# Rotary tables that carry the row factors, and values transposed by DMA in a one-layer convolution and retention kernel

## The chip, the cores and the metric

The kernel runs on one core of one Trainium2 chip. A core has five engines that each run their own instructions in order and wait for one another through semaphores: PE (matrix products, with its weight loads shown apart as PEld), DVE (vector operations), ACT (element-wise functions and copies), POOL (a second, slower vector engine) and SP, which here only issues transfers (DMAs). SBUF is the memory on the chip that all of them work in, PSUM the banks that PE writes. The metric is the device time of one execution in microseconds. Three runs of the kernel before took 887.11, 887.15 and 887.49 us; the median is 887.15.

## The reference

One layer of a hybrid mixer over 2064 rows (16 learned "meta" rows, then 2048 input rows) of 1024 features. Four heads of chunked retention and four groups of gated convolution share one input projection and one output projection.

```python
def mixer_layer(h, norm_g, w_in, conv_w, ret_norm_g, w_out, pos):
    hn = rms_norm(h, norm_g)
    proj = jnp.einsum('bld,de->ble', hn, w_in)
    cx, cb, cc, cg, q, k, v, rg = jnp.split(proj, N_PROJ, axis=-1)
    conv_out = short_conv_branch(cx, cb, cc, conv_w) * jax.nn.silu(cg)
    qf = rotary(q.reshape(shp), pos) * (RET_HEAD_DIM ** -0.5)
    kf = rotary(k.reshape(shp), pos)
    ret = head_group_norm(retention_chunkwise(qf, kf, vf), ret_norm_g)
    ret_out = ret * jax.nn.silu(rg)
    mixed = jnp.concatenate([conv_out, ret_out], axis=-1)
    return h + jnp.einsum('ble,ed->bld', mixed, w_out)
```

In retention, a chunk of 128 rows has `scores = (q k^T) * decay`, an inner part `scores v`, a cross part from a running state, and the state gets `k^T v` of the chunk. `head_group_norm` then takes away each row's mean and divides by its spread, with a small constant EPS under the root. A last RMS norm closes the layer. `rms_norm` divides a row by the root of its mean square: that factor, one number a row, is called the row factor below.

## The kernel before

**Rows and passes.** The 2048 rows are worked in two passes (`r` = 0, 1) of 1024 rows; a pass has two halves (`j` = 0, 1) of 512. Everything is kept with features in the 128 partitions and rows along the free axis. The row factor isn't applied to the input; it is put in later, where it is cheap.

**Products.** A "unit" is one head or one convolution group. Each unit has two "quads". A quad computes two feature tiles (128 features) for both halves. `quad` (lines 206 to 241) does it with seven products instead of eight, in Strassen's manner: sums of weights on one side, sums of inputs on the other, three banks. Each product is 12 matmuls, since each operand is split into a rounded part and a rest (`mh`/`ml` for the inputs, `wh`/`wl` for the weights). After products 0, 2 and 3 ACT copies a bank (`copy`, L222, tile `tc`); `take` then gets what belongs to tile `i` (0 or 1) and half `j`: for three of the four a bank and a copy that DVE adds, for the last, `take(1, 0, xb, None)`, a bank alone. Where the summed inputs aren't ready yet, `quad_plain` (L254) does eight plain products.

**Feeding PE.** SP loads four raw weight tiles (`ra`, eight buffers, L439), POOL makes the sums (`sa`, `ra`, L111 and L114), ACT casts each to `wh` (L102), DVE subtracts to get `wl` (L114). `wh` and `wl` have three buffers each, so the cast for a product can run once the product three before it has left PE.

**A head** (`head`, L596). The first quad gives keys and values: `take` (L603) writes `kv` tiles and turns the keys with `rotary` (L571), four DVE instructions that read the tables `rot_t`. The second quad gives queries, turned likewise, and gates (tile `qg`), which are multiplied by the row factor and put through Silu. Then, for each half: PE transposes the keys chunk by chunk (L654), ACT scales them to `kd` (L656), PE transposes the values (L659), ACT writes them back times the squared row factor (L663), PE makes the state updates (L669). After that scores (L682), the decay mask (L684), inner and cross parts (L692, L693) and the group norm follow. A normalised tile `y` is turned to the feature layout by `turn` (L714): ACT splits 32-bit words into two planes of 16 bits (L716), a transposing DMA moves the planes (L717, `across<-apart`), and later ACT joins them (`finish`, L722). `turn` and `finish` wait in two lists and are worked off by `catch_up` in the two quads of the next unit, each tied behind a bank copy.

**What sets the order.** The program is written unit by unit, and a list scheduler that simulates the engines orders the instructions of each engine ahead of time; `tc.issue_after(ins)` puts what is in its block behind `ins` on the same engine. The order on an engine is then fixed, and a late instruction holds up all that follow it there. The tiles `kv`, `qg`, `u`, `x`, `t` and others share 16 buffers (`gen`).

**Row factors.** `row_factors` (L347) sums squares on ACT; `spread_factors` (L326) makes the factor `rc` (POOL's power, L281), spreads it over the partitions with a diagonal and PE (`spread`, L284, tile `rot`, L295) into `rr` and, squared, `rr2`, and returns the square `rc2` by row and `ev`, the EPS term of the group norm. In the first pass this happens while plain products run, just ahead of the first head.

Of the kernel before, what the change touches and what calls it, by code (L numbers as in the profile page):

```python
# [15 lines left out]
P = 128  # L16
# [55 lines left out]
def hybrid_trunk(ctx: ExitStack, tc: tile.TileContext, t, out: bass.AP, chunk_decay):  # L72
# [132 lines left out]

    def quad(w, m, take):


        def product(i, bank, first):
            (wh, wl) = w[i]  # L210
            for kt in range(KH):
                ks = slice(kt * P, (kt + 1) * P)
                mh, ml = m[i][kt]
                for n, (a, b) in enumerate(((wl, mh), (wh, ml), (wh, mh))):
                    nc.tensor.matmul(  # L215
                        bank, a[:, ks], b, start=first and kt == 0 and n == 0, stop=kt == KH - 1 and n == 2,
                        skip_group_check=not first,
                    )

        def copy(bank):  # L220
            c = sb.tile([P, HB], F32, name="tc", tag="tc", bufs=COPIES)
            copied[0] = nc.scalar.copy(out=c, in_=bank)  # L222
            return c

        xb = ps_proj()
        product(0, xb, True)
        c = copy(xb)
        yb = ps_proj()
        product(1, yb, True)
        take(0, 0, yb, c)  # L230
        product(2, xb, False)
        u2 = copy(xb)
        zb = ps_proj()
        product(3, zb, True)
        c = copy(zb)
        product(4, xb, False)
        take(1, 1, xb, c)
        product(5, zb, False)
        take(0, 1, zb, u2)
        product(6, xb, False)  # L240
        take(1, 0, xb, None)
# [84 lines left out]
    def spread_factors(ss, rr, rr2):  # L326
# [3 lines left out]
        rc = small.tile([P, CH], F32, name="rc", tag="rc")  # L330
        v = rsqrt_mean(rc, ss[:, 0, :])
        spread(rc, P, rr, rr2)
        rc2 = small.tile([P, CH], F32, name="rc2", tag="rc2", bufs=2 * NR)
        nc.vector.tensor_tensor(out=rc2, in0=rc, in1=rc, op=ALU.mult)
# [3 lines left out]
            in0=eps_col.rearrange("p (h c) -> p h c", c=1).broadcast_to([P, NG, CH]),  # L338
            in1=v.rearrange("p (h c) -> p h c", h=1).broadcast_to([P, NG, CH]),
            op=ALU.mult,  # L340
        )
        return rc2, ev

# [239 lines left out]
    def planes(a):  # L583
        return a.bitcast(U16).rearrange("p (two n) -> p two n", two=2)

    waiting = [[], []]

# [8 lines left out]
    def head(h, r, m, rot_t, f, turning, blocks, ahead, first=(), between=()):  # L596


        between = iter(between)
        k, v = [None, None], [None, None]  # L600
        tables = [rot_t[:, :, j * HB : (j + 1) * HB] for j in range(2)]

        def take(i, j, pp, c):  # L603
            d = gen("kv")[:, :HB]
            if c is None:
                nc.scalar.copy(out=d, in_=pp)
            else:
                add(nc.vector, d, pp, c)
            if i == 0:
                rotary(d, tables[j])  # L610
                k[j] = d
            else:
                v[j] = d

        if len(first) > 0:
# [7 lines left out]
        def take(i, j, pp, c):  # L623
# [8 lines left out]
            else:  # L632
# [3 lines left out]
                nc.vector.tensor_tensor(out=d, in0=pp, in1=f[0][:, j * HB : (j + 1) * HB], op=ALU.mult)  # L636
                nc.scalar.activation(d, d, AF.Silu)
                sg[j] = d
# [3 lines left out]
        else:  # L642
            quad(stationary(load_raw(w_loads(2 * h + 1))), m, take)
            catch_up(1)
        next(between, lambda: None)()
        if blocks[1]:
# [4 lines left out]
        for j in range(2):  # L651
# [4 lines left out]
            nc.scalar.mul(kd, tp, kd_col[:, h : h + 1])  # L656
            tp = ps_misc()
            for c in range(CH):
                nc.tensor.transpose(tp[:, c * P : (c + 1) * P], v[j][:, c * P : (c + 1) * P], ident)  # L659
            vj = v[j]  # L660
            for c in range(CH):
                cs = slice(c * P, (c + 1) * P)
                nc.scalar.mul(vj[:, cs], tp[:, cs], f[2][j][0][:, c : c + 1])  # L663
            vt.append(vj)
# [13 lines left out]
        for j in range(2):  # L678
# [22 lines left out]
            rs = small.tile([P, CH, 1], F32, name="rs", tag="rs")  # L701
            ev = f[2][j][1]
            add(nc.vector, rs, mv[:, :, 1:2], ev[:, h, :].rearrange("p (c a) -> p c a", a=1))
# [9 lines left out]

            def turn(j=j, y=y, apart=turning[0][:, j * HB : (j + 1) * HB], across=turning[1][:, j * HB : (j + 1) * HB]):  # L714

                nc.scalar.copy(out=planes(apart), in_=halves(y))  # L716
                nc.sync.dma_start(  # L717
                    across.bitcast(U16).rearrange("p (c f) -> p c f", c=2 * CH), apart.bitcast(U16), transpose=True
                )

# [94 lines left out]
    for r in range(NR):  # L815
# [4 lines left out]
        def load_tables():  # L820
            nc.sync.dma_start(rot_t, t["rot"][:, :, p0 : p0 + BLK])

        if r == 0:
            w = [None] * 4
# [21 lines left out]
            for _ in row_factors(0, f):  # L846
                pass
            nc.sync.dma_start(causal, t["causal"])
            nc.sync.dma_start(conv_w, t["conv_w"])
# [9 lines left out]
        else:  # L859
            m, b = moving(load_x(r), gain_of)  # L860
            first = [plain_parts(w_loads(0))]
            load_tables()
            prepared(m, sums_x, (1, 3))
            between = (lambda: prepared(m, sums_x, (0, 2)),)
# [75 lines left out]
```

## Time and profile before

| | |
|---|---|
| median of three runs | 887.15 us |
| the profiled execution | 886.64 us |
| its span, first to last instruction | 884.9 us |
| DMA queue 1, share of 16 engines | 43.0% |
| mean granted PE clock | 0.999 |

In the rows that the prediction shows, a group is "line engine operation out<-in shapes xcount | busy us, mean ns of one | idle time just before them, and what ended it". A row of the timeline is "start, length, engine, line, operation, count, and in brackets the idle time before it". A row of the chain of waits is "start, length, what", and each piece is the work that the next piece had to wait for. PE's matmuls overlap in the pipeline: a matmul's own length is longer than the step from one to the next.

### The profile page before, as it was taken

The page shows a single profiled execution, that of the slowest core. Times are in us where ns is not written, and L with a number is a line of the kernel's source. Part 1 is how long each engine was busy: PE and PEld are TensorE (multiplying, and loading weights), DVE is VectorE, ACT ScalarE, POOL GpSimd, SP SyncE. Part 2 cuts the span into 40 slices and gives each one's busy share as a digit, 9 for nine tenths or more (in the row PEclk, how much of TensorE's full clock was granted, in tenths as well). Part 3 has the DMA queues.
Part 4 walks back from the last instruction along what each step waited for, and adds up shares of the span by engine and source line. Part 5 has one row for each costly group of instructions (what it writes and reads, how often), then busy time and mean ns, then how long its engine had stood idle before and what let it go on. Part 6 is the DMA issues. An engine that isn't in the chain of part 4 may idle for free.

```text
span 884.9 us, 12802 instructions
## 1 busy us (share of the span) xinstructions
PE 872.3 (99%) x4343; PEld 717.7 (81%) x4343; DVE 718.4 (81%) x1176; ACT 441.1 (50%) x848; POOL 400.4 (45%) x291
## 2 busy tenths in 40 slices
PE   8999999999999999999999999999999999999996
PEld 5778788878888878888888888888888887788885
DVE  6888888989877866999899999877768699767763
ACT  8664426354545463836352534444334475555553
POOL 0554232323235554452223333354546445887773
PEclk9999999999999999999999999999999999999999
DMA  9721216455334343834236363325222493545531
GB/s 338 234 65 50 73 49 180 142 152 170 90 101 145 107 144 95 288 113 135 58 85 215 88 223 96 119 71 155 60 72 60 145 366 108 175 159 175 171 129 74
DMA packets 93137, 121.12 MB, mean 137 GB/s; under 512 B 24528, under 2 KB 41232, under 8 KB 93072
## 3 DMA queue, kind: packets, MB, share of 16 engines
q1 hardware_dynamic: 93072, 120.31, 43.0%
q8 instruction: 34, 0.56, 0.3%
q14 instruction: 31, 0.25, 0.1%
HBM read 90.92 MB, written 25.17 MB: 131 GB/s over the span
## 4 chain that ended last, share of the span: by engine, by line
PE 56%; DVE 6%; DMA 2%; issue 2%; ACT 1%; POOL 1%; SPq 0%; POOLq 0%; DVEq 0%; ACTq 0%
PE pj L215 50%; DVE ml L114 2%; PE pj L265 2%; DVE wl L114 1%; PE ms L682 1%; PE ms L669 1%; DVE ml L106 1%; PE ms L693 1%; PE ms L692 1%; DMA t<-sums_w 1%; DMA n<-in_x 1%; POOL yo L111 0%; DMA yo<-in_x 0%; DMA ra<-in_w_in 0%; DVE pm L709 0%
## 5 line engine op out<-in xcount | busy, mean ns | idle before, releaser
L215 PE MATMUL pj<-mh,wl 128*128 128x512 f32 x1008 | 398.7, 396 | 1.9 <-ACT tc L222 1.0
L215 PE MATMUL pj<-ml,wh 128*128 128x512 f32 x1008 | 393.2, 390 | 0.0
L215 PE MATMUL pj<-mh,wh 128*128 128x512 f32 x1008 | 392.7, 390 | 0.0
L102 ACT CAST wh<-ra 128x512 fp32r<-128x512 f32 x216 | 133.7, 620 | 260.9 <-PE pj L215 201.3
L215 PEld LDWEIGHTS pj<-mh,wl 128*128 128x128 f32 x1008 | 189.3, 188 | 44.7 <-ACT tc L222 2.8
L114 DVE TENSOR_TENSOR wl<-ra,wh 128x512 fp32r<-128x512 f32 x216 | 193.4, 898 | 39.3 <-ACT wh L102 38.9
L215 PEld LDWEIGHTS pj<-mh,wh 128*128 128x128 f32 x1008 | 189.2, 188 | 39.8
L215 PEld LDWEIGHTS pj<-ml,wh 128*128 128x128 f32 x1008 | 189.4, 188 | 37.9 <-issue 0.5
L114 POOL TENSOR_TENSOR ra<-ra 128x512 f32<-128x512 f32 x72 | 113.1, 1571 | 93.9 <-PE ms L400 40.9
L111 POOL TENSOR_TENSOR sa<-ra 128x512 f32<-128x512 f32 x36 | 55.2, 1533 | 100.0 <-DVE wl L114 46.7
L114 POOL TENSOR_TENSOR ra<-sa,ra 128x512 f32<-128x512 f32 x36 | 52.5, 1459 | 92.5 <-DVE wl L114 78.2
L222 ACT COPY tc<-pj 128x512 f32<-128x512 f32 x108 | 62.8, 581 | 0.0
L265 PE MATMUL pj<-ml,mh 128*128 128x512 f32 x128 | 50.2, 392 | 0.1
L265 PE MATMUL pj<-mh,mh 128*128 128x512 f32 x128 | 49.9, 393 | 0.0
L265 PE MATMUL pj<-mh,ml 128*128 128x512 f32 x128 | 48.8, 398 | 0.5 <-DVE ml L114 0.4
L525 POOL TENSOR_TENSOR c<-c,rr 128x512 f32<-128x512 f32 x14 | 27.8, 1984 | 26.8 <-DVE c L525 18.0
L705 POOL TENSOR_TENSOR rp<-rs,neg_half 128x4 f32<-128x4 f32 x16 | 19.4, 1215 | 43.4 <-DVE rs L111 43.4
L756 DVE TENSOR_TENSOR yo<-pj,yo 128x512 f32<-128x512 f32 x32 | 21.9, 687 | 17.9 <-PE pj L215 8.0
L102 ACT CAST wh<-sa 128x512 fp32r<-128x512 f32 x36 | 22.4, 621 | 27.5 <-PE pj L215 27.4
L761 POOL TENSOR_TENSOR z<-yo,final_g 128x512 f32<-128x512 f32 x16 | 27.0, 1687 | 16.1 <-DVE yo L756 16.1
L525 POOL TENSOR_TENSOR c<-c,tc 128x512 f32<-128x512 f32 x14 | 25.5, 1823 | 17.8 <-ACT tc L552 17.8
L758 ACT ACTIVATE rot<-yo 128x512 f32<-128x512 f32 x32 | 20.2, 630 | 26.8 <-DVE yo L756 25.8
(137 smaller groups left out, 1166.0 us busy)
## 6 DMA issues: line engine op xcount, KB each, us to landing
ra<-in_w_in SPq DMA_DIRECT2D x128, 256.0 KB, 2.7
x<-in_xT SPq DMA_DIRECT2D x48, 256.0 KB, 4.8
w<-in_w_out SPq DMA_DIRECT2D x32, 256.0 KB, 4.7
ra<-mixed SPq DMA_DIRECT2D x32, 256.0 KB, 2.9
yo<-in_x SPq DMA_DIRECT2D x32, 256.0 KB, 4.6
ra<-in_x SPq DMA_DIRECT2D x16, 256.0 KB, 3.2
mixed<-c SPq DMA_DIRECT2D x16, 256.0 KB, 2.5
mixed<-qg SPq DMA_DIRECT2D x16, 256.0 KB, 2.4
```

What stands on the lines that cost most here:

```text
L102: nc.scalar.copy(out=hi, in_=src)
L106: nc.vector.scalar_tensor_tensor(out=lo, in0=src, scalar=scale, in1=hi.bitcast(F32), op0=ALU.mult, op1=ALU.subtract)
L111: eng.tensor_tensor(out=out, in0=a, in1=b, op=ALU.add)
L114: eng.tensor_tensor(out=out, in0=a, in1=b, op=ALU.subtract)
L215: nc.tensor.matmul(bank, a[:, ks], b, start=first and kt == 0 and n == 0, stop=kt == KH - 1 and n == 2, skip_group_check=not first,)
L222: copied[0] = nc.scalar.copy(out=c, in_=bank)
L265: nc.tensor.matmul(banks[i], a[:, ks], b, start=half + kt + n == 0, stop=half == 1 and kt == KH - 1 and n == 2,)
L525: eng.tensor_tensor(out=out, in0=a, in1=b, op=ALU.mult)
L705: nc.gpsimd.tensor_tensor(out=rp, in0=rs, in1=neg_half.rearrange("p (c a) -> p c a", a=1), op=ALU.pow)
L756: last[0] = nc.vector.tensor_tensor(out=y, in0=pp, in1=y, op=ALU.add)
L758: nc.scalar.activation(junk, y, AF.Square, accum_out=ss[:, i, j : j + 1])
L761: nc.gpsimd.tensor_tensor(out=ys[i][j], in0=y, in1=final_g[:, j * HB : (j + 1) * HB], op=ALU.mult)
```

## The change

Three things are done together.

1. `scale_tables` multiplies both rotary tables by the squared row factor `rr2`, in place, on POOL, once a pass and half. Keys and queries so carry the squared row factor from the rotary on. For the keys this stands in for the factor that the values had; for the queries it is one number a row, and the group norm takes it out again, with `ev` now made from `rc2`.
2. The values need no factor any more, and PE no longer transposes them. `part` splits a value tile into planes on ACT (tile `pl`), and a transposing DMA moves it (tile `tr`). The value tile of half 0 is split right from its bank, in `take`; that of half 1 is first added up by DVE and then split behind the second quad's first bank copy (`split_late`). `join` puts the planes together on ACT (tile `v`): half 0 behind the second quad's second copy, half 1 behind its last copy. At the second pass's first head, whose first quad is plain, both are split from their banks.
3. The gates' Silu moves from the second quad to `turn`, in the next unit.

```diff
-    def quad(w, m, take):
+    def quad(w, m, take, steps=()):
+        steps = iter(steps)
...
+        def step():
+            with tc.issue_after(copied[0].ins):
+                next(steps, lambda: None)()
+
         xb = ps_proj()
         product(0, xb, True)
         c = copy(xb)
+        step()
...
         product(2, xb, False)
         u2 = copy(xb)
+        step()
...
+    def cross(across, apart):
+        nc.sync.dma_start(
+            across.bitcast(U16).rearrange("p (c f) -> p c f", c=2 * CH), apart.bitcast(U16), transpose=True
+        )
+
+    def part(a):
+        apart, across = gen("pl")[:, :HB], gen("tr")[:, :HB]
+        nc.scalar.copy(out=planes(apart), in_=halves(a))
+        cross(across, apart)
+        return across
...
         def take(i, j, pp, c):
+            if i == 1 and c is None:
+                v[j] = part(pp)
+                return
...
-                nc.scalar.activation(d, d, AF.Silu)
...
-            quad(stationary(load_raw(w_loads(2 * h + 1))), m, take)
+            def split_late():
+                for j in late:
+                    v[j] = part(v[j])
+
+            def join(j):
+                a = gen("v")[:, :HB]
+                nc.scalar.copy(out=halves(a), in_=planes(v[j]))
+                v[j] = a
+
+            quad(stationary(load_raw(w_loads(2 * h + 1))), m, take, (split_late, lambda: join(0)))
             catch_up(1)
+            with tc.issue_after(copied[0].ins):
+                join(1)
...
-            tp = ps_misc()
-            for c in range(CH):
-                nc.tensor.transpose(tp[:, c * P : (c + 1) * P], v[j][:, c * P : (c + 1) * P], ident)
             vj = v[j]
-            for c in range(CH):
-                cs = slice(c * P, (c + 1) * P)
-                nc.scalar.mul(vj[:, cs], tp[:, cs], f[2][j][0][:, c : c + 1])
...
+                nc.scalar.activation(sg[j], sg[j], AF.Silu)
...
+        def scale_tables():
+            for j in range(2):
+                a = rot_t[:, :, j * HB : (j + 1) * HB]
+                b = f[1][:, j * HB : (j + 1) * HB].rearrange("p (a n) -> p a n", a=1)
+                nc.gpsimd.tensor_tensor(out=a, in0=a, in1=b.broadcast_to([P, 2, HB]), op=ALU.mult)
```

In the first pass `scale_tables()` stands behind `row_factors`, in the second behind `load_tables()`.

How the instructions move on an engine is shown at three places. On PE, after the second quad of the first pass's first head (`ms` is a PSUM bank, `ident` the identity of the transposes, `pj` a product's bank), before:

```order
L215 MATMUL pj<-mh_358,wh 128x512
L400 MATMUL ms<-ra,meta_s 16x128 x8
L654 MATMUL ms<-ident,kv 128x128 x4
L659 MATMUL ms<-ident,kv 128x128 x4
L215 MATMUL pj<-mh_115,wl 128x512
```

And now, where the keys' transposes are L688 and a product is L217:

```order
L217 MATMUL pj<-mh_358,wh 128x512
L408 MATMUL ms<-ra,meta_s 16x128 x8
L688 MATMUL ms<-ident,kv 128x128 x4
L217 MATMUL pj<-mh_115,wl 128x512
L217 MATMUL pj<-ml_116,wh 128x512
```

The four value transposes between the keys' and the next product are gone; the same holds at all 16 such places.

On POOL, ahead of the first pass's first head (`rc` is the power of the second half's row factors, `u` and `carry` belong to the convolution, `sa` and `ra` are the weight sums of the head's first quad), before:

```order
L111 TENSOR_TENSOR sa<-ra 128x512
L281 TENSOR_TENSOR rc<-rs_v,neg_half 128x4
L454 COPY u<-u 128x2
L453 COPY u<-carry_78 128x2
L114 TENSOR_TENSOR ra<-ra 128x512
L456 COPY carry_78<-u 128x2
L114 TENSOR_TENSOR ra<-sa,ra 128x512
```

And now:

```order
L111 TENSOR_TENSOR sa<-ra 128x512
L289 TENSOR_TENSOR rc<-rs_v,neg_half 128x4
L855 TENSOR_TENSOR rot_t<-rot_t,rr_363 128x2x512
L462 COPY u<-u 128x2
L461 COPY u<-carry_78 128x2
L114 TENSOR_TENSOR ra<-ra 128x512
L855 TENSOR_TENSOR rot_t<-rot_t,rr_363 128x2x512
L464 COPY carry_78<-u 128x2
L114 TENSOR_TENSOR ra<-sa,ra 128x512
```

The two table multiplies stand ahead of the weight sum `ra<-sa,ra`.

On SP, at the second pass's first head (`mixed` is a store of the unit before, `t` are summed inputs for products 3 and 4 of the head's second quad, counted from 0), before:

```order
L447 DMA mixed_89<-c 128x4x128
L447 DMA mixed_88<-c 128x4x128
L439 DMA ra<-in_w_in 128x512
L201 DMA t<-sums_x 128x512 x8
L439 DMA ra<-in_w_in 128x512 x7
```

And now:

```order
L455 DMA mixed_89<-c 128x4x128
L455 DMA mixed_88<-c 128x4x128
L595 DMA_TRANSPOSE tr<-pl 128x8x128
L447 DMA ra<-in_w_in 128x512
L595 DMA_TRANSPOSE tr<-pl 128x8x128
L201 DMA t<-sums_x 128x512 x8
L447 DMA ra<-in_w_in 128x512 x7
```

Both value transposes stand ahead of the eight loads.

More of the change, by code (lines that the diff above doesn't have):

```diff
@@ L330, in spread_factors @@
         rc = small.tile([P, CH], F32, name="rc", tag="rc")
-        v = rsqrt_mean(rc, ss[:, 0, :])
+        rsqrt_mean(rc, ss[:, 0, :])
         spread(rc, P, rr, rr2)
-        rc2 = small.tile([P, CH], F32, name="rc2", tag="rc2", bufs=2 * NR)
+        rc2 = small.tile([P, CH], F32, name="rc2", tag="rc2")
         nc.vector.tensor_tensor(out=rc2, in0=rc, in1=rc, op=ALU.mult)
@@ L338, in spread_factors @@
             in0=eps_col.rearrange("p (h c) -> p h c", c=1).broadcast_to([P, NG, CH]),
-            in1=v.rearrange("p (h c) -> p h c", h=1).broadcast_to([P, NG, CH]),
+            in1=rc2.rearrange("p (h c) -> p h c", h=1).broadcast_to([P, NG, CH]),
             op=ALU.mult,
         )
-        return rc2, ev
+        return ev
     def row_tile(name, pair):
@@ L599, in head @@
         between = iter(between)
-        k, v = [None, None], [None, None]
+        k, v, late = [None, None], [None, None], []
         tables = [rot_t[:, :, j * HB : (j + 1) * HB] for j in range(2)]
         def take(i, j, pp, c):
+            if i == 1 and c is None:
+                v[j] = part(pp)
+                return
             d = gen("kv")[:, :HB]
@@ L613, in take @@
                 v[j] = d
+                late.append(j)
         if len(first) > 0:
@@ L701, in head @@
             rs = small.tile([P, CH, 1], F32, name="rs", tag="rs")
-            ev = f[2][j][1]
+            ev = f[2][j]
             add(nc.vector, rs, mv[:, :, 1:2], ev[:, h, :].rearrange("p (c a) -> p c a", a=1))
@@ L716, in turn @@
                 nc.scalar.copy(out=planes(apart), in_=halves(y))
-                nc.sync.dma_start(
-                    across.bitcast(U16).rearrange("p (c f) -> p c f", c=2 * CH), apart.bitcast(U16), transpose=True
-                )
+                cross(across, apart)
+                nc.scalar.activation(sg[j], sg[j], AF.Silu)
                 def finish():
@@ L847, in hybrid_trunk @@
                 pass
+            scale_tables()
             nc.sync.dma_start(causal, t["causal"])
@@ L862, in hybrid_trunk @@
             load_tables()
+            scale_tables()
             prepared(m, sums_x, (1, 3))
```

## The prediction

> **What bounds the kernel now.** I read the page's first part (busy time by engine), the chain of waits by engine, and the chain in order of time around one head.
>
> ```profile
> PE 872.3 (99%) x4343; PEld 717.7 (81%) x4343; DVE 718.4 (81%) x1176; ACT 441.1 (50%) x848; POOL 400.4 (45%) x291
> PE 56%; DVE 6%; DMA 2%; issue 2%; ACT 1%; POOL 1%; SPq 0%; POOLq 0%; DVEq 0%; ACTq 0%
> L102 ACT CAST wh<-ra 128x512 fp32r<-128x512 f32 x216 | 133.7, 620 | 260.9 <-PE pj L215 201.3
> ```
>
> PE (the matrix engine) is busy 99% of the span. The third row says which way the waiting goes: ACT, which casts the weights for PE, sits idle 201.3 us because PE has not yet released one of the three weight buffers. The feeders wait for PE. So an instruction taken off PE is worth its time on PE, as long as what feeds PE is not made later. What one transpose is worth on PE is read from the chain, at the second head pass (columns: start, length, what):
>
> ```profile
> 404.62 0.44 PE ms L654 x4
> 405.06 0.44 PE ms L659 x4
> 405.50 5.46 PE pj L215 x24
> ```
>
> Four value transposes (L659) take 0.44 us, so one takes 0.11 us; a product matmul takes 5.46/24 = 0.2275 us, and a product of 12 takes 2.73 us.
>
> **The change part by part.** These groups (busy time, mean ns of one) and this transfer row price the edits:
>
> ```profile
> L659 PE MATMUL ms<-ident,kv 128*128 128x128 f32 x64 | 10.1, 272 | 0.0
> L663 ACT ACTIVATE kv<-ms,rc 128x128 f32<-128x128 f32 x64 | 18.3, 372 | 0.0
> L606 ACT COPY kv<-pj 128x512 f32<-128x512 f32 x11 | 6.3, 586 | 12.1 <-PE pj L215 8.2 <-PE pj L265 3.6
> L716 ACT COPY apart<-pm 128x1024 uint16<-128x1024 uint16 x16 | 16.7, 1045 | 20.4 <-DVE pm L709 20.4
> L722 ACT COPY apart<-across 128x1024 uint16<-128x1024 uint16 x16 | 20.6, 1354 | 0.0
> across<-apart SPq DMA_TRANSPOSE x16, 3.1
> ```
>
> *Value transposes removed.* 64 leave PE. The mean of 272 ns is no price, because transposes overlap: 64 x 272 ns would be 17.4 us, the busy time is 10.1 us, and the chain, which counts only what the next instruction waits for, gives 64 x 0.11 = **7.0 us off the span**. I take that.
>
> [...]
>
> *ACT.* It loses 64 row-factor multiplies (18.3 us) and nine of the eleven L606 copies (9 x 0.59 = 5.3 us; the two that write keys at the head with plain products stay). It gains 16 split copies and 16 joins: 16 x (1.05 + 1.35) = 38.4 us by L716 and L722, the same operations on another tile; a split that reads PSUM is not in the trace, and I hold it between L606's 0.59 and twice L716, 2.1 us, taking 1.05. Net +15 us on an engine idle half the span: 0 on the path. The cover is the wait of 201.3 us above; a cast may come nearly two products (5.46 us) after its buffer is free. The Silu only moves to the next unit.
>
> *Joins.* The first value's transfer starts when the first quad ends. The first join stands behind the second quad's second copy, three products, 8.2 us later. A split (1.05), the issue and the landing (3.1) fit. The second join follows the third copy, and PE uses the values only after the quad. Cost 0 there.
>
> *Row factors into the tables, first pass.* Two new POOL (GpSimd) multiplies of 1024 elements a row. The trace has only 512 at a time:
>
> ```profile
> 45.27 0.68 DVE L114 TENSOR_TENSOR ml<-x,mh 128x512 fp32r<-128x512 f32 x1
> 45.88 1.78 DVE L114 TENSOR_TENSOR wl<-ra,wh 128x512 fp32r<-128x512 f32 x1
> 50.15 0.68 DVE L288 TENSOR_TENSOR rot<-ident,rc 128x512 f32<-128x512 f32 x1
> 45.70 1.41 POOL L111 TENSOR_TENSOR sa<-ra 128x512 f32<-128x512 f32 x1 [0.36 <-ACT mh L102]
> 47.88 1.34 POOL L281 TENSOR_TENSOR rc<-rs_v,neg_half 128x4 f32<-128x4 f32 x1 [0.77 <-DVE rs_v L278]
> 51.59 1.02 PE L295 MATMUL ms<-rot,ones 128*128 128x512 f32 x2
> L114 POOL TENSOR_TENSOR t<-x 128x512 f32<-128x512 f32 x4 | 12.9, 3236 | 9.3 <-DVE x L175 9.3
> ```
>
> POOL's sum at 45.70 and DVE's (VectorE's) subtraction at 45.88 did not run side by side: DVE finished at 47.66, 0.55 us after POOL's end at 47.11, and POOL itself ran from DVE's previous end (45.95) for 1.16 us. So a 1024-element multiply should hold DVE for 2 x 1.16 = 2.3 us. The first one stands right behind the power that ends at 49.22; DVE then owes PE the diagonal `rot`, which ends at 50.83 and is used at 51.59, 0.76 us of slack. Held 2.3 us, PE loses 2.3 - 0.76 = 1.5 us; with DVE going first (the last row: POOL needed 3.2 us where DVE ran back to back) it loses 0. Call it A, 0 to 1.5; the nearest row is the held subtraction, so **A = 1.5 us**.
>
> [...]
>
> The second multiply stands in front of the sum that PE needs for product 2:
>
> ```profile
> 55.78 1.35 POOL L114 TENSOR_TENSOR ra<-ra 128x512 f32<-128x512 f32 x1
> 57.07 1.46 POOL L456 COPY carry<-u 128x2 f32<-128x2 f32 x1
> 58.49 1.28 POOL L114 TENSOR_TENSOR ra<-sa,ra 128x512 f32<-128x512 f32 x1
> 59.81 0.62 ACT L102 CAST wh<-ra 128x512 fp32r<-128x512 f32 x1 [2.40 <-POOL ra L114]
> 60.34 0.58 ACT L489 COPY cb<-pj 128x512 f32<-128x512 f32 x1
> ...
> 61.87 0.61 ACT L102 CAST wh<-sa 128x512 fp32r<-128x512 f32 x1
> 62.38 0.59 ACT L222 COPY tc<-pj 128x512 f32<-128x512 f32 x1
> 63.01 0.50 PE L215 MATMUL pj<-mh,wl 128*128 128x512 f32 x1 [0.63 <-ACT tc L222]
> ```
>
> Before: POOL ends 59.77, the cast starts 59.81, the bank copy ends 62.97, PE goes on at 63.01. In the changed order the three instructions from 60.34 to 61.87 stand ahead of the cast, so PE goes on 3.24 - 1.53 = 1.7 us after POOL's end. That end moves by 2 x 1.28 = 2.6 us to 62.4: PE at 64.1, **B = +1.1 us**. Between +0.2 (the 1.46 us copy, which took 0.58 elsewhere, shrinks) and +2.0 (each half at 1.75, POOL's slow form).
>
> *Second pass tables.* The same two multiplies near 331 and 337 us, 60 us ahead of their use. DVE is held 2.3 us, less than one product; 0, at most 1.0.
>
> *SP (the transfer queue), start of the second pass.* The second value transpose stands ahead of eight loads that feed products 3 and 4 (counted from 0) of the next quad:
>
> ```profile
> 396.63 3.98 SPq L201 DMA_DIRECT2D t<-sums_x  x8
> 398.58 1.27 ACT L606 COPY kv<-pj 128x512 f32<-128x512 f32 x2 [3.64 <-PE pj L265]
> 401.55 0.62 ACT L102 CAST mh<-t 128x512 fp32r<-128x512 f32 x1 [1.18 <-DMA t<-sums_x]
> 411.10 1.29 DVE L114 TENSOR_TENSOR ml<-t,mh 128x512 fp32r<-128x512 f32 x2
> 412.72 5.46 PE pj L215 x24
> t<-sums_x SPq DMA_DIRECT2D x16, 256.0 KB, 4.1
> L717 SPq DMA_TRANSPOSE across<-apart x16: 1232/1237/1358, 124.3 to 584.3; - x16
> ```
>
> That transpose waits for ACT's second split, now ending about 400.3 (second half of the 1.27 us pair, plus 1.05 for 0.59), and takes 1.24 us to issue: the loads start at 401.6 instead of 396.63, 5.0 us later, the first landing at 405.7. ACT then works through six casts, two weight casts, the key scaling and the bank copy (about 0.52 us each: done near 411.0), the join (412.3) and the last two casts. PE, 0.44 us earlier than before, wants that bank copy near 410.4 and the joined values near 411.9. **C = 0.6 + 0.4 = 1.0 us**; 0 if the loads land in 3.1 us as the first did, 2.5 if the last pieces (then done near 414, against 412.39 before) hold product 4.
>
> **Sum** against the profiled run: span 884.9 - 7.0 + 1.5 + 1.1 + 1.0 = 881.5; with the 1.7 us around the span 883.2 against 886.64. The median shown, 887.15, lies 0.5 us above the profiled run, so **883.7**.
>
> **The rivals.**
> (1) *Nothing is given back*: DVE goes ahead of POOL, and the loads land quickly. 887.15 - 7.0 = 880.1. For it: the 3.2 us row; against it: POOL stands on the path at 59.77 already.
> (2) *The gain is eaten*: A 1.5, B 2.0, C 2.5 and 1.0 in the second pass, 7.0 us in all: 887.15, no change. For it: all four add work to a queue that PE then waits on; against it: the upper ends would have to meet.
> (3) *Transposes land late and ACT stands at the join*, with the weight casts behind it. The transfer starts about 2.4 us into the quad (split 1.05, the other transpose's issue 1.24). Landing in 3.1 us it has 2.7 us to spare at 8.2. A later one is covered for another 5.46 - 0.62 - 0.69 = 4.1 us (two products less a cast and a subtraction), so it costs from a landing of 9.9 us, and then 8 us for each us, once a head: 0.6 us above that gives 883.7 + 4.8 = 888.5, no change. Against it: the row of 16 such transfers says 3.1.
> [...]
> (4) *Slower: SP's queue delays the weights.* In the first pass PE itself reads the raw weights at the end of a head:
>
> ```profile
> 188.32 0.33 SPq L439 DMA_DIRECT2D ra<-in_w_in  x1
> 192.64 0.63 PE L400 MATMUL ms<-ra,meta_s 128*16 128x128 f32 x16
> ra<-in_w_in SPq DMA_DIRECT2D x128, 256.0 KB, 2.7
> ```
>
> The last load lands near 191.0, 1.6 us before use. If two more transposes push it by their issue and one landing (2.48 + 3.1 = 5.6 us), PE stands 4.0 us at each of four heads: 883.7 + 16 = 899.7. It is slower than before by over 0.2% from a push of 2.9 us. Against it: the new transposes stand ahead of the head's first two loads, while the last two wait for DVE to free their buffers.
>
> **How the numbers follow.** 0.2% is 1.8 us, about what a measurement of this kernel can tell from no change. Chances: forecast 0.54, (1) 0.18, (2) 0.17, (3) 0.03, (4) 0.08. Faster than 885.4: the forecast but for its upper edge, (1), and a little of (2): 0.75. Within 0.2%: 0.17. Slower: 0.08. The range runs from just under (1), 879.8, to just over (2), 887.3. The likeliest case alone spans 881.5 to 886.
>
> **What would show it.** Right: 64 fewer PE matmuls; PE busy lower by about 10 us; stalls of 1 to 3 us in all on PE between 50 and 66 us, with POOL's table multiply or ACT's bank copy as the releaser; ACT casts of `t` about 5 us later near 405. Wrong: no PE stall there (rival 1), `v<-tr` copies waiting for DMA (rival 3), L408 waiting for `ra` (rival 4).

## The result and the profile after

| | before | after |
|---|---|---|
| median | 887.32 us (6 runs) | 892.52 us (6 runs, 890.1 to 895.0) |
| the profiled execution | 886.64 us | 890.1 us |
| its span | 884.9 us | 888.3 us |
| ratio of the times, 95% interval | | 1.0059 (1.0040 to 1.0079) |

The changed kernel is slower by 0.6%. The forecast was 883.7, 0.4% faster, with a range that ended at 887.3. The profiled execution of the changed kernel is the lowest of its six, 2.4 us under their median; a part of that goes with the granted clock, which is told at the end.

The totals by engine, from the first part of the page of the changed kernel, and its group of weight casts (columns as before):

```profile
PE 866.5 (98%) x4279; PEld 711.6 (80%) x4279; DVE 719.4 (81%) x1176; ACT 455.1 (51%) x807; POOL 404.7 (46%) x295
L102 ACT CAST wh<-ra 128x512 fp32r<-128x512 f32 x216 | 133.8, 620 | 269.7 <-PE pj L217 222.6
```

64 matmuls are gone, as announced, and PE is busy 5.8 us less; but the span is 3.4 us longer. Call the time from the start of one PE instruction to the start of the next a step, and the median of steps of the same kind its usual length. The steps that are over 0.1 us longer than usual are too long by 12.8 us in all before and by 23.3 us now. So 7.0 us went out and some 10.5 us of new waits came in. ACT's casts wait for PE even more than before (222.6 against 201.3 us): that sum, on which the forecast leaned, got better while the kernel got slower.

**Where in the program.** The second pass begins with plain products, L265 before and L273 now. Here is the first of them in the PE timeline of the kernel before:

```profile
374.18 0.39 PE L265 MATMUL pj<-mh,ml 128*128 128x512 f32 x1
```

And in that of the changed kernel:

```profile
378.93 0.39 PE L273 MATMUL pj<-mh,ml 128*128 128x512 f32 x1
```

Half of the transposes stood in each pass, worth 3.5 us each by the chain. Yet the first pass is 4.75 us *longer* than before, and the second (884.9 - 374.18 = 510.7 before, 888.3 - 378.93 = 509.4 now) only 1.3 us shorter. The new waits are these, in order of time.

*Ahead of the first head, the first table multiply.* Rows of the timeline:

```profile
49.98 2.60 POOL L855 TENSOR_TENSOR rot_t<-rot_t,rr 128x1024 f32<-128x1024 f32 x1
50.25 2.88 DVE L483 TENSOR_TENSOR u<-u,rr 128x512 f32<-128x512 f32 x1
53.05 0.68 DVE L296 TENSOR_TENSOR rot<-ident,rc 128x512 f32<-128x512 f32 x1
53.78 1.12 PE L303 MATMUL ms<-rot,ones 128*128 128x512 f32 x2 [1.43 <-DVE rot L296]
```

A DVE product of 512 elements that takes 0.68 us elsewhere takes 2.88 us beside POOL's 2.60, the diagonal `rot` is late, and PE's step ahead of L303 is 1.6 us too long.

*The second multiply, and what it delays:*

```profile
60.08 4.25 POOL L855 TENSOR_TENSOR rot_t<-rot_t,rr 128x1024 f32<-128x1024 f32 x1
60.20 0.67 DVE L483 TENSOR_TENSOR cb<-cb,rr 128x512 f32<-128x512 f32 x1
60.80 1.27 DVE L114 TENSOR_TENSOR ml<-t,mh 128x512 fp32r<-128x512 f32 x2
64.42 1.26 POOL L114 TENSOR_TENSOR ra<-sa,ra 128x512 f32<-128x512 f32 x1
65.71 0.62 ACT L102 CAST wh<-ra 128x512 fp32r<-128x512 f32 x1 [4.17 <-POOL ra L114]
66.36 1.21 DVE L114 TENSOR_TENSOR wl<-ra,wh 128x512 fp32r<-128x512 f32 x1 [4.29 <-ACT wh L102]
67.72 0.47 PE L217 MATMUL pj<-mh,wl 128*128 128x512 f32 x1 [3.04 <-DVE wl L114]
```

Here DVE went on at its usual pace until 62.07 (60.80 + 1.27), and POOL needed 4.25 us, 2.26 of them after that; the chain POOL, ACT, DVE, PE behind it stands row under row. PE's step is 3.2 us too long, against 0.8 at this place before.

*In the heads of the first pass*, PE waits for the decayed scores `pm`, which DVE makes:

```profile
169.84 0.49 PE L720 MATMUL ms<-v,pm 128*128 128x128 f32 x2 [0.73 <-DVE pm L712]
220.64 0.49 PE L720 MATMUL ms<-v,pm 128*128 128x128 f32 x2 [2.32 <-DVE pm L712]
```

The brackets hold PE's wait. By steps it is 0.9 and 2.5 us, against nothing and 0.6 before. The forecast knew nothing of this place.

*At the start of the second pass*, ACT's casts of the summed inputs come late, and in a bunch:

```profile
409.31 0.62 ACT L102 CAST mh<-t 128x512 fp32r<-128x512 f32 x1 [1.57 <-DMA t<-sums_x]
411.91 2.57 ACT L102 CAST mh<-t 128x512 fp32r<-128x512 f32 x4
414.90 0.58 ACT L224 COPY tc<-pj 128x512 f32<-128x512 f32 x1
415.26 0.50 PE L217 MATMUL pj<-ml,wh 128*128 128x512 f32 x1 [1.14 <-DVE ml L114]
```

PE's step is 1.3 us too long here, and 0.5 at 423. *At the first convolution group of the second pass* ACT stands 4.4 us at a Silu, with PE's bank copy queued behind it:

```profile
565.58 1.36 ACT L672 COPY v<-tr 128x1024 uint16<-128x1024 uint16 x1
...
600.64 0.63 ACT L560 ACTIVATE tc<-tc 128x512 f32<-128x512 f32 x1 [4.38 <-DVE tc L533]
601.18 0.60 ACT L102 CAST wh<-ra 128x512 fp32r<-128x512 f32 x1
601.68 0.57 ACT L224 COPY tc<-pj 128x512 f32<-128x512 f32 x1
602.31 0.50 PE L217 MATMUL pj<-mh,wl 128*128 128x512 f32 x1 [1.32 <-ACT tc L224]
```

That is 1.5 us, where there was none before. (The first row is the last head's second join, of which more below.)

### The profile page after: what moved, and what is told of

It is laid out like the page before. It is cut to its first block, busy times and chain, and to the rows that moved or that the text cites. A ratio compares the mean times of both kernels' runs of the same rounds, so it can differ in the third digit from the quotient of the medians.

```text
span 888.3 us, 12659 instructions
## 1 busy us (share of the span) xinstructions
PE 866.5 (98%) x4279; PEld 711.6 (80%) x4279; DVE 719.4 (81%) x1176; ACT 455.1 (51%) x807; POOL 404.7 (46%) x295
## 5 line engine op out<-in xcount | busy, mean ns | idle before, releaser
L217 PE MATMUL pj<-mh,wl 128*128 128x512 f32 x1008 | 397.8, 395 | 6.2 <-DVE wl L114 3.9
L217 PE MATMUL pj<-ml,wh 128*128 128x512 f32 x1008 | 392.6, 389 | 1.1 <-DVE ml L114 1.1
L217 PE MATMUL pj<-mh,wh 128*128 128x512 f32 x1008 | 393.1, 390 | 0.0
L102 ACT CAST wh<-ra 128x512 fp32r<-128x512 f32 x216 | 133.8, 620 | 269.7 <-PE pj L217 222.6
L114 DVE TENSOR_TENSOR wl<-ra,wh 128x512 fp32r<-128x512 f32 x216 | 189.9, 881 | 47.7 <-ACT wh L102 47.1
L217 PEld LDWEIGHTS pj<-mh,wl 128*128 128x128 f32 x1008 | 189.3, 188 | 49.0 <-ACT tc L224 7.3
L217 PEld LDWEIGHTS pj<-mh,wh 128*128 128x128 f32 x1008 | 189.2, 188 | 39.9
L217 PEld LDWEIGHTS pj<-ml,wh 128*128 128x128 f32 x1008 | 189.4, 188 | 39.6 <-DVE ml L114 1.6
L111 POOL TENSOR_TENSOR sa<-ra 128x512 f32<-128x512 f32 x36 | 52.8, 1466 | 87.5 <-DMA ra<-in_w_in 22.9
L273 PE MATMUL pj<-ml,mh 128*128 128x512 f32 x128 | 50.4, 394 | 0.1
L273 PE MATMUL pj<-mh,mh 128*128 128x512 f32 x128 | 50.1, 394 | 0.0
L273 PE MATMUL pj<-mh,ml 128*128 128x512 f32 x128 | 49.0, 400 | 0.2
```

The source lines that it names most:

```text
L102: nc.scalar.copy(out=hi, in_=src)
L111: eng.tensor_tensor(out=out, in0=a, in1=b, op=ALU.add)
L114: eng.tensor_tensor(out=out, in0=a, in1=b, op=ALU.subtract)
L217: nc.tensor.matmul(bank, a[:, ks], b, start=first and kt == 0 and n == 0, stop=kt == KH - 1 and n == 2, skip_group_check=not first,)
L273: nc.tensor.matmul(banks[i], a[:, ks], b, start=half + kt + n == 0, stop=half == 1 and kt == KH - 1 and n == 2,)
```

## The experiments

The theory after this reading: (T1) the transposes are worth 7.0 us, and tables, queue and order give it back; the rival (T2): in the first pass PE isn't the only bound, so the transposes are worth less there whatever replaces them. Each time below is a median, with its ratio to runs of the kernel before on the same chip. The six runs of the changed kernel lie between 890.1 and 895.0 us, so a gain over their median of 892.52 is uncertain by some 2 us.

### 1. The value transposes left out, nothing in their place

To the kernel before:

```diff
-            tp = ps_misc()
-            for c in range(CH):
-                nc.tensor.transpose(tp[:, c * P : (c + 1) * P], v[j][:, c * P : (c + 1) * P], ident)
             vj = v[j]
-            for c in range(CH):
-                cs = slice(c * P, (c + 1) * P)
-                nc.scalar.mul(vj[:, cs], tp[:, cs], f[2][j][0][:, c : c + 1])
```

> The kernel before, with the value transposes on PE and their row-factor multiplies on ACT left out and nothing in their place (the state updates and inner parts read the values as they are, so this part is not computed). If the transposes are worth what the chain of waits says, 64 x 0.11 us: 887.3 - 7.0 = 880.3. If PE merely waits elsewhere once they are gone (DVE, busy 81%, is next): 884 or more.

Measured: 883.95 us against 887.36, ratio 0.9965 (0.9951 to 0.9979): **3.4 us, not 7.0**. The second pass begins here:

```profile
375.04 0.39 PE L265 MATMUL pj<-mh,ml 128*128 128x512 f32 x1
```

That is 0.9 us *later* than the 374.18 of before, although 32 transposes (3.5 us) ahead of it are gone. The second pass takes 881.2 - 375.04 = 506.2 us against 510.7, 4.5 less. So the second pass paid in full, and the first pass paid nothing. These are PE's new waits there:

```profile
106.80 0.47 PE L215 MATMUL pj<-mh,wl 128*128 128x512 f32 x1 [1.13 <-DVE wl L114]
165.92 0.49 PE L686 MATMUL ms<-kv,pm 128*128 128x128 f32 x2 [0.74 <-DVE pm L678]
216.12 0.49 PE L686 MATMUL ms<-kv,pm 128*128 128x128 f32 x2 [1.71 <-DVE pm L678]
288.78 0.50 PE L215 MATMUL pj<-mh,wl 128*128 128x512 f32 x1 [1.42 <-ACT tc L222]
```

Three of four end with DVE. The last ends with ACT, which there works off the squares of loaded rows, in the same queue. By steps the four grew by 0.9, 0.9, 1.3 and 1.1 us over what they were before, 4.2 in all, of which 3.1 end with DVE. T2 holds, for the first pass.

### 2. The table multiplies alone

`scale_tables` and its two calls are added to the kernel before; nothing else changes.

> The kernel before, plus the four table multiplies on POOL at the places they have in the changed kernel; the values keep PE's transposes and their own factor (so the keys carry the factor once too often). If the two PE stalls of 1.6 and 3.2 us near 52 and 64 us belong to the multiplies: 1.6 + (3.2 - 0.8) = 4.0 us, 887.3 + 4.0 = 891.3. If they belong to the rest of the change: 887.3. By the prediction's sizes (1.5 + 1.1): 889.9.

Measured: 891.93 us, ratio 1.0044 (1.0031 to 1.0056): **4.6 us slower** (3.9 by the ratio), near the 4.0 of the stalls and over the 2.6 of the forecast. But in this profile the time isn't lost where it was expected. The first stall is 2.4 us instead of 1.6, and PE's step near 68 us is only 1.1 us too long, 0.3 more than in the kernel before. PE came there later, and POOL's second multiply took 2.45 us instead of 4.25. DVE paused for 0.55 us when it had just started, and then took 2.27 us for its product:

```profile
60.98 2.45 POOL L828 TENSOR_TENSOR rot_t<-rot_t,rr 128x1024 f32<-128x1024 f32 x1
61.70 2.27 DVE L475 TENSOR_TENSOR cb<-cb,rr 128x512 f32<-128x512 f32 x1 [0.55 <-ACT cb L489]
```

Behind the first stall the granted clock halves; windows of 1 us (start:end, length, then busy time of PE, PEld, DVE, ACT, POOL; the first figure behind POOL is PE's granted clock):

```profile
54.00:55.00 1.00, 0.24 (x1) 0.24 (x2) 1.00 (x4) 0.00 (x0) 0.58 (x1) 1.00 0.00 0
55.00:56.00 1.00, 1.00 (x3) 0.18 (x2) 1.00 (x3) 0.59 (x2) 0.00 (x0) 0.85 0.00 0
56.00:57.00 1.00, 1.00 (x21) 0.79 (x25) 1.00 (x2) 1.00 (x4) 0.00 (x0) 0.50 0.00 0
57.00:58.00 1.00, 1.00 (x21) 0.50 (x13) 1.00 (x3) 1.00 (x4) 0.00 (x0) 0.50 0.00 0
58.00:59.00 1.00, 1.00 (x3) 0.81 (x4) 1.00 (x4) 0.96 (x5) 0.00 (x0) 0.50 0.00 0
59.00:60.00 1.00, 1.00 (x6) 0.82 (x5) 1.00 (x4) 0.52 (x2) 0.88 (x2) 0.95 0.00 0
```

PE lost 0.15 + 3 x 0.5 + 0.05 = 1.7 us of full clock here, after having stood still. The two stalls and the clock make 2.4 + 0.3 + 1.7 = 4.4 of the 5.2 us by which this execution's span is longer than before. The other four runs took 891.0 to 892.1 us at mean clocks of 0.997 and 0.998, so the time doesn't hang on this half clock; where they lost it was not profiled. That the sum comes near the 4.0 expected is partly luck.

### 3. The change without the tables

Both calls of `scale_tables` are taken out of the changed kernel.

> The changed kernel without the table multiplies (the row factor is left out of keys and values). If the multiplies cost 4.0 us: 892.5 - 4.0 = 888.5, and PE's stall near 64 us back at 0.8. What then stays above 880.3 (8.2 us) belongs to the DMA transposes and the moved work on ACT, SP and DVE. If the multiplies cost nothing: 892.5.

Measured: 886.75 us, ratio 0.9997 (0.9988 to 1.0006). That is 5.8 us under the changed kernel, more than the two stalls of 4.0; PE's step near 62 us is back at 0.95. It is also 2.8 us above experiment 1, which has neither transposes nor anything for them: the price of transfers, splits, joins and the moved Silu. With that, the change in three parts: transposes -3.4 (experiment 1), their replacement +2.8 (3 against 1), tables +4.6 to +5.8 (2 against before, 3 against after). Each is a difference of medians, and uncertain by 1 to 2 us.

### 4. The tables later

In the changed kernel the multiplies go behind a weight sum of the first head's first quad (and in the second pass to the head's start):

```diff
-        sub(nc.gpsimd, a11, s1, a11)
+        summed[0] = nc.gpsimd.tensor_tensor(out=a11, in0=s1, in1=a11, op=ALU.subtract)
...
+            w = stationary(blocks[0])
+            if h == 0:
+                with tc.issue_after(summed[0].ins):
+                    scale_tables()
```

> The changed kernel with both table multiplies of a pass put behind POOL's weight sum ra<-sa,ra of the first head's first quad (in the second pass, at the head's start). Nothing is left out. If POOL's order is the cause of the stalls near 52 and 64 us, both go: 892.5 - 4.0 = 888.5. If two-input work of POOL beside DVE costs the same wherever it stands: 892.5.

Measured: 889.42 us, ratio 1.0021 (1.0011 to 1.0030), 3.1 us better than the change. The stall near 52 us is gone, and that of product 2 is back at 0.9 us; but one of 1.4 us stands at the next product. So most of it was the place on POOL, and a part is the multiplies themselves: 5.20 us of POOL for the two, beside DVE, whose subtractions take 2.2 to 2.9 us there.

### 5. The Silu back in the second quad

> The changed kernel with the gates' Silu back in the second quad, right behind the gates' row factor. Nothing is left out. If the moved Silu, which now stands on ACT behind the split of a turned tile, makes the new 1.5 us stall at the second pass's first convolution group and lengthens the heads' stalls: 892.5 - 1.5 = 891.0 or less. If it costs nothing, as the prediction put it: 892.5.

Measured: 890.05 us, ratio 1.0037 (1.0024 to 1.0049): 2.5 us better, but not where it was expected. The stall near 600 us stays at 1.5 us. It is the heads that gain: the wait of 0.9 us at 169 is gone, and that of 2.5 us near 220 is 1.1, while one near 110 us grew by 0.6, which makes 1.7 us net. The spans of the two profiled executions, both without a half clock up to 870 us, differ by 1.6 us (888.3 and 886.7). So "the Silu only moves" was not free. By which chain the moved Silu delays `pm` was not tried apart.

### 6 and 7. DVE's load in the heads, with a control

`prepare`, DVE's work on inputs of the second pass, is written in two steps behind each of heads 1 and 2 of the first pass. Here it moves behind the first two convolution groups that follow the heads; in 6 with the transposes left out, in 7 to the kernel before alone.

```diff
-                if unit > 0:
+                if unit > 0 and r > 0:
                     next(later, None)
                     next(later, None)
...
+                if r == 0:
+                    next(later, None)
+                    next(later, None)
```

> The first experiment (value transposes left out, nothing in their place) with one thing moved: the first pass prepares the summed inputs of the second pass (DVE's lines 175 and 114 on x tiles) in its convolution groups instead of in heads 1 to 3, where DVE was busy 90% of the time. If DVE, once PE has less to do, is what ends the first pass's heads: the stalls there go and the whole 7.0 us comes: 880.3. If the lost 3.6 us has another cause: 884.0 as in the first experiment.

> Control: the kernel before with the same preparation moved, and nothing else. If DVE doesn't end the heads while PE still has the transposes: 887.3 (at most 0.6 us less, the one stall of the heads there). If the move is a gain by itself: 884 or less.

Measured: 884.94 us, ratio 0.9968 (0.9956 to 0.9980), and for the control 890.91, ratio 1.0034 (1.0021 to 1.0046). Both expectations missed: the move costs 3.3 us by itself, with stalls of 1.7, 0.7 and 1.8 us in the convolution groups. But the difference of the two says what was asked: with DVE's work out of the heads, leaving out the transposes is worth 890.91 - 884.94 = **6.0 us**, against 3.4 with it there, and PE's waits for `pm` at 165 and 216 us are gone.

### 8. The loads ahead of the second transpose

At the second pass's first head the second value transpose is issued behind the last load of the summed inputs (`loaded[0]`; `go` issues the transfer that `part` has put aside in `later`):

```diff
+        for go in later:
+            with tc.issue_after(loaded[0].ins):
+                go()
```

> The changed kernel with the second value transpose of the second pass's first head issued behind the eight loads of summed inputs instead of ahead of them. Nothing is left out. If the loads' place is what PE waits for near 414 us: the stalls of 1.3 and 0.5 us there go, 892.5 - 1.8 = 890.7. If ACT's longer list (splits, joins) is the cause: 892.5.

Measured: 889.85 us, ratio 1.0026 (1.0016 to 1.0037), 2.7 us better than the change. PE's busy time in the window from 410 to 415 us, first the change, then this kernel (columns as above):

```profile
410.00:415.00 5.00, 4.12 (x18) 3.03 (x17) 4.92 (x7) 4.74 (x9) 0.72 (x1) 1.00 0.96 325
```

```profile
410.00:415.00 5.00, 5.00 (x26) 4.12 (x25) 4.77 (x6) 4.50 (x10) 3.30 (x2) 1.00 0.54 138
```

Both stalls there are gone. The loads' place in the queue was the cause, as the forecast said, and it was worth 1.8 us by the stalls; the rest of the 2.7 is within the uncertainty.

### 9. The second join early

The second join is written behind the third bank copy, inside the quad, instead of behind the quad:

```diff
         c = copy(zb)
+        step()
         product(4, xb, False)
...
-            quad(stationary(load_raw(w_loads(2 * h + 1))), m, take, (split_late, lambda: join(0)))
+            quad(stationary(load_raw(w_loads(2 * h + 1))), m, take, (split_late, lambda: join(0), lambda: join(1)))
             catch_up(1)
-            with tc.issue_after(copied[0].ins):
-                join(1)
```

> The changed kernel with the second join tied behind the second quad's third bank copy, written ahead of that quad's last three products instead of behind them. Nothing is left out. In the changed order ACT takes that join some four products late, and PE's state updates of the second half with it; if this lateness, which pushes the last head's group norm into the first convolution group of the second pass, makes the stall of 1.5 us near 600 us, it goes: 892.5 - 1.5 = 891.0. If the stall comes from DVE's and POOL's conflicts alone: 892.5.

Measured: 891.69 us, ratio 1.0053 (1.0039 to 1.0066), 0.8 us better, which can't be told from no change. In the last head of the second pass the two joins now start at 556.12 and 558.80 us, where the changed kernel had the second at 565.58. Near 600 us the stall is gone; from 595 to 606 us PE is busy all the time:

```profile
595.00:606.00 11.00, 11.00 (x50) 9.00 (x49) 8.89 (x11) 5.96 (x10) 7.33 (x5) 1.00 0.20 58
```

In the changed kernel the same window has 9.68. So the late join was the cause there. But the earlier order makes two new waits, in heads of the second pass:

```profile
489.18 0.49 PE L719 MATMUL ms<-v,pm 128*128 128x128 f32 x2 [0.54 <-DVE pm L711]
536.11 0.49 PE L719 MATMUL ms<-v,pm 128*128 128x128 f32 x2 [0.56 <-DVE pm L711]
```

So the waits moved, and no gain is shown.

### 10 and 11. All mends together

Tables behind both weight sums that the first quad needs soonest, loads first, Silu back; in 10 with the early join, in 11 without.

> All mends together: the table multiplies behind both of the weight sums that the first head's first quad needs soonest, the loads of summed inputs ahead of the second value transpose, the Silu back in the second quad, the second join early. Nothing is left out. If the single gains (3.1, 2.7, 2.5, and 1.5 for the stall near 600 us) add up: 892.5 - 9.8 = 882.7, below the kernel before. If they are partly the same time (DVE is the next bound in the first pass): 886 to 888.

> The mended kernel without the early join. Nothing is left out. If the single gains add up: 892.5 - 8.3 = 884.2. If not: 887 to 889.

Measured: 887.13 us, ratio 1.0003 (0.9994 to 1.0012), and **886.17 us, ratio 0.9986 (0.9977 to 0.9994)**. The second is just faster than the kernel before, by 0.14%. The single gains don't add up: 8.3 us were expected of three mends, 6.4 came, though both are uncertain by some 2 us. The early join costs 1.0 us here (10 against 11).

### 12 to 14. DVE's work spread thinly

The control of 7 was itself slower, so the question of 6 was put again with a gentler move: `prepare` does one step behind each of heads 1, 2, 3 and the next convolution group, instead of two behind each of heads 1 and 2.

> Control: the kernel before with the preparation of summed inputs in the first pass spread out, one step (three multiplies with subtraction and one subtraction on DVE) behind each of heads 1, 2, 3 and the convolution group that follows, instead of two steps behind heads 1 and 2. Nothing is left out. If DVE doesn't bound PE in the kernel before: 887.3, within 0.6.

> The first experiment (value transposes left out) with the preparation spread in the same way. If DVE in the heads took 3.6 of the 7.0 us, and the stalls of the sixth experiment's control came only from crowding the convolution groups: 881 to 882, with the stalls of 0.9 and 1.9 us in the heads smaller or gone. If the heads lose it whatever DVE does: 884.

> The mended kernel (tables later, loads first, Silu back) with the preparation spread in the same way. Nothing is left out. If the heads' stalls there (0.5, 0.6 and 1.3 us between 190 and 217 us) are DVE's: 886.2 - 2.4 = 883.8. If not: 886.2.

Measured: the control 887.32 us, ratio 1.0001 (0.9992 to 1.0010), no change, as expected; without transposes 882.65, ratio 0.9947 (0.9933 to 0.9960), **4.7 us gained** where experiment 1 gained 3.4; mended 886.05, ratio 0.9985 (0.9977 to 0.9994), no better than 11. The heads, 98 to 284 us, in windows (PE's busy time is the figure behind the length): experiment 1, then experiment 13.

```profile
98.00:284.00 186.00, 182.42 (x1051) 152.02 (x1040) 162.55 (x332) 78.89 (x139) 66.50 (x49) 1.00 0.42 125
```

```profile
98.00:284.00 186.00, 184.88 (x1074) 154.51 (x1074) 160.42 (x329) 80.47 (x145) 67.15 (x50) 1.00 0.41 120
```

PE stands 3.6 us in experiment 1 and 1.1 in experiment 13: the stalls at `pm` go with DVE's load. What is left is the wait for `wl` near 107 us, in the first head, ahead of which no `prepare` stands; DVE runs back to back there in both. But part of what was won is lost behind the heads, where ACT works off the row squares: the stall there is 2.1 us, against 1.6 in experiment 1 and 0.5 before. So the whole 7.0 us never came, and the expected 881 to 882 was missed by 0.7 us.

## Why the prediction was wrong

**The step that failed first: "an instruction taken off PE is worth its time on PE", 64 x 0.11 = 7.0 us.** It is worth 3.4 (experiment 1). The removed work is 7.0 us, as the chain said: the second pass became 4.5 us shorter, its 3.5 and a little more. In the first pass the gain was zero: DVE stands right behind PE in the heads, which took 3.1 us back, and ACT behind the heads took 1.1. The row on which the step rested, ACT's 201.3 us of waiting for PE, is a sum over the whole span and over one feeder that runs three buffers ahead. It says nothing of DVE's `pm`, which can't run ahead: it needs PE's scores and gives PE's next operand. Nor does DVE's busy share show it. Here are a window over a head of the first pass and one over the second pass's heads, in the kernel before (start:end, length, then busy time of PE, PEld, DVE):

```profile
196.00:246.00 50.00, 49.57 (x288) 41.21 (x290) 45.20 (x92) 23.23 (x44) 14.22 (x11) 1.00 0.45 139
460.00:500.00 40.00, 40.00 (x210) 34.08 (x209) 37.15 (x77) 16.96 (x30) 13.63 (x8) 1.00 0.53 171
```

DVE was busy 90% of the first and 93% of the second, and yet the second pass paid in full. What differs is how long `pm` lay ready before PE used it. In both windows:

```profile
214.71 0.75 DVE L684 SCALAR_TENSOR_TENSOR pm<-ms,cols,causal 128x512 f32<-128x512 f32 x1
215.50 0.49 PE L692 MATMUL ms<-kv,pm 128*128 128x128 f32 x2 [0.43 <-DVE pm L684]
...
472.06 0.75 DVE L684 SCALAR_TENSOR_TENSOR pm<-ms,cols,causal 128x512 f32<-128x512 f32 x1
475.19 0.38 PE L692 MATMUL ms<-kv,pm 128*128 128x128 f32 x2
```

It is 0.04 us near 215, where PE already had a step 0.6 us too long, and 2.4 us near 473. In the kernel before it is under 0.1 us at the first `pm` of heads 1 and 2 of the first pass, the two places where the new waits for `pm` arose, and 1.2 us or more in all heads of the second pass. With `prepare` spread out (experiment 13) it is 0.4 and 1.7 us at those two places, against 0.05 in experiment 1. Why the second pass has slack at a higher busy share was not tried. PE's busy time, too, fell by 5.8 and not by the 10 us of the forecast, which had taken the group's row there.

**A and B, the table multiplies: mechanism right, size too small.** 1.5 + 1.1 were forecast; 4.6 came when they were added alone. A was 1.6 in the profile of the change and 2.4 in that of experiment 2. B was mis-sized in one term: 2 x 1.28 us for the second multiply, which took 4.25 in the change, beside DVE running back to back, so that B was 3.2 - 0.8 = 2.4; in experiment 2 the multiply took 2.45, near the forecast, PE itself came later, and B was 0.3. The forecast quoted just this case (POOL's 3.2 us for half as much) as a reason for A being zero, and not as B's price. The two are one coin: at the first multiply (2.60 us) DVE's product took 2.88 us instead of 0.68, and at the second DVE's kept its 0.67 and POOL's multiply took 4.25. It also priced the stall alone, and not the half clock (3.41 us at 0.50) that followed the one of 2.4 us in experiment 2.

**C, the loads behind the second transpose: right place and cause,** 1.0 forecast, 1.8 by the stalls, 2.7 by the medians of experiment 8.

**"Joins: cost 0" and "the Silu only moves": wrong.** Neither made anything wait for a transfer, as the forecast said. But the order on ACT and PE shifted: the second join came some 7 us late, and with it the state updates, the scores and the group norm of a head, which ran into the next unit's work (the stall of 1.5 us that experiment 9 takes away, though an earlier join makes other waits). The Silu's new place cost 1.7 us in the heads by the steps, 2.5 by the medians (experiment 5). "ACT idle half the span" covered the busy time, not the places.

**Second-pass tables, 0:** PE has no new stall near them. Of the rivals, (3) (late transposes) and (4) (late raw weights) did not happen: PE does not wait at L408, nor ACT at a join for a transfer. The 0.6 us by which (3) put the landing over 9.9 us are shown by no run: in the changed kernel the 16 value transposes landed 2.7 to 3.9 us after their issue, 3.0 at the median. (2) had the right idea, a gain eaten by several waits, but stopped at 7.0 us because it took the gain for whole.

The sum as the runs have it: -3.4 for the transposes, +2.8 for what replaces them, +4.6 for the tables, +4.0, against +5.2 measured. The 1.2 us left over lies between experiments 2 and 3 (tables 4.6 on the old order, 5.8 on the new one), and is within what such medians differ by.

## What to carry to other kernels

Before pricing work taken off the busiest engine, look at what it takes from the other engines in the same stage, above all where the two must alternate (PE, DVE, PE): how long does the operand lie ready before it is used? Where that slack was nothing here (under 0.1 us), or a wait stood there already, the gain was eaten; the busy share of the other engine didn't tell (90% in the stage that gave nothing, 93% in the one that paid in full). And price a POOL operation beside DVE both ways: here it was once DVE's product that was late (2.88 us instead of 0.68) and once POOL's multiply (4.25 us instead of 2.60).

## What the hardware showed that was not expected

**Behind six of PE's 12 long stalls the clock was halved, and where they lay in time told them from the other six.** In the 16 profiled executions of this study, the kernel before among them, PE had 12 stalls of 2.0 us or more, by steps. Behind six of them the granted clock was 0.50 for 3.41 us, which is 1.7 us of full clock, among them the 2.4 us of experiment 2 shown above; behind the other six, among them the 3.2 and 2.5 us of the changed kernel, it stayed at 1.00. The traces' record of the clock tells them apart. The six stretches at 0.50 last 3.413 us each, and the stretches at 1.00 just ahead of them 47.79, 211.63, 3.41, 61.44, 279.89 and 283.31 us, which is 14, 62, 1, 18, 82 and 83 times 3.413. So in these executions the clock changed on a grid of 3.413 us, and this grid did not lie at the same times in each: by the windows the half clock begins at 55.7 us in experiment 2 and at 67.0 in experiment 9, 3.3 cells later. In the grid cell ahead of each half clock PE's steps were too long by 2.14 to 2.77 us in sum; in every other cell at full clock, up to 870 us, by 2.11 at most. Here is the stall of 3.2 us near 67 us, first in experiment 9, then in the changed kernel, each with the two cells that it touches (columns as in experiment 2):

```profile
63.60:67.00 3.40, 0.77 (x4) 0.31 (x2) 0.97 (x1) 1.62 (x4) 3.02 (x4) 1.00 0.00 0
67.00:70.40 3.40, 3.01 (x7) 2.46 (x8) 3.35 (x6) 0.52 (x2) 0.05 (x1) 0.50 0.35 96
```

```profile
62.60:66.00 3.40, 2.08 (x10) 1.39 (x8) 0.00 (x0) 0.29 (x1) 3.32 (x4) 1.00 0.00 0
66.00:69.40 3.40, 1.68 (x8) 1.43 (x9) 3.01 (x4) 1.85 (x4) 1.02 (x1) 1.00 0.09 30
```

In experiment 9 all but 0.4 us of it lies in one cell, and the next runs at half clock; in the changed kernel a line of the grid cuts it, and the clock stays. PE was not idle throughout the cell ahead of the half clock: in experiment 9 it was busy for 0.77 of the 3.40 us shown.

The runs agree with such losses in part. One half clock of 3.41 us lowers the mean granted clock by 0.002. In experiment 3 the five runs at 0.998 took 886.15 to 886.45 us, the six at 0.995 and 0.996 took 886.75 to 888.55. Of the changed kernel's six, those at 0.993 and 0.992 took 895.0 and 894.3 us, but of the two at 0.998 one took 890.1 and one 892.0. Where the clock fell in runs that were not profiled was not seen.

**POOL's multiply of 1024 elements took 2.60 us with DVE's product at 2.88, and 4.25 us beside DVE's run.** In the first case POOL's recorded start (49.98) lies 0.27 us ahead of that of DVE's product (50.25), which took 2.88 us instead of 0.68. In the second it (60.08) also lies ahead of that of DVE's next product (60.20), by 0.12 us, yet that product took its usual 0.67 us and it was POOL's multiply that was late. Here the recorded start did not tell which of the two would be late.
